# PSUM banks of the mixers dealt out anew: three for the projections, three for the HGRN, two for the mLSTM

## The chip, the cores and the metric

The kernel runs on one core of one Trainium2 chip. TensorE (PE) multiplies matrices and writes its results to PSUM, a memory of eight banks of 128 x 512 float32 each. VectorE (DVE) and ScalarE (ACT) read them from there; GpSimd (POOL) works on SBUF alone, and SyncE (SP) starts DMAs. The metric is the device time of one execution in microseconds; less is better. Where several runs were made their median is given.

## The reference

One residual block of a streaming encoder, 1024 tokens of width 1024, all in float32. What matters here is its first part, a mixer of two head groups that share one input projection:

```python
u = x @ w_in[i] + b_in[i]
hq, hf, hv, hgate, mq, mk, mv, mo, mig, mfg = _split_cols(u)
...
o_hg = hgrn2_mixer(silu(hq), log_f, k_hg, hv)            # 4 heads, 128 x 128 state
o_hg = head_rms_norm(o_hg, hg_norm_g[i]) * silu(hgate)
...
h_ml = mlstm_mixer(mq_c, mk_c, mv, mig, log_sigmoid(mfg)) # 4 heads, qk 64, v 128
o_ml = head_rms_norm(h_ml, ml_norm_g[i]) * sigmoid(mo)
mix = concatenate([o_hg, o_ml], -1) @ w_out[i]
x = layer_norm(ALPHA * x + mix, ln1_g[i], ln1_b[i])
```

Of the mLSTM, one step over a chunk of tokens is:

```python
qk = einsum('bhtd,bhsd->bhts', q_, k_) * w_intra
num = einsum('bhts,bhsv->bhtv', qk, v_) + w_inter[..., None] * einsum('bhtd,bhdv->bhtv', q_, C_st)
den = sum(qk, -1) + w_inter * einsum('bhtd,bhd->bht', q_, n_st)
h = num / maximum(abs(den), exp(-m_t))[..., None]
...
C_new = w_old[..., None, None] * C_st + einsum('bhs,bhsd,bhsv->bhdv', ws, k_, v_)
```

After the mixer come a SwiGLU feed-forward layer with its own layer norm and a gated embedding.

## The kernel before

The kernel goes through four stages: the mixers (`mixers`, up to about 416 us of the span), the output projection with the first layer norm (`out_proj`), and the two halves of the feed-forward layer with the last gate (`ffn_up`, `ffn_down`). All projections are done in three matmuls per product (`mm3`, lines 88 to 90): each float32 operand is split into a high part and the rest, and high x high, high x rest and rest x high are added up in PSUM.

The mixers use all eight PSUM banks, dealt out in three groups by `bank(tag, shape, name)`: `ft` for the projections, `hg` for the HGRN, `ml` for the mLSTM. A tile that is asked for takes a free bank of its group; its first writer waits until the bank's former tile has been read for the last time.

Projections (`ft`): `f_tile` computes one 128-column tile of the projection for 512 tokens at a time, 24 matmuls into one bank, and then calls an `evac` that reads the bank (ACT and DVE). `tok_group` does the same for 256 columns of two token tiles, with one DVE addition (L250) as the reader. `hf_tile` reads its bank twice on ACT (L489, L490), `hq_tile` once on ACT and once on DVE (L503, L504), the gates at the end once on ACT (L634).

Between them runs the recurrent work, as Python generators. `f_tile` and `tok_group` call `pump()` in the middle and at the end of each group, and each call moves every stream on to its next `yield`. So in the code the PE work of the streams stands between groups of 12 or 24 projection matmuls.

The mLSTM (`ml`, lines 407 to 468) takes eight chunks of 128 tokens, one after the other, and for each chunk asks for seven banks (six in the last): two `pq` (scores, L425, read by L427), `pk` (transposed keys, L430, read by L432); after a `yield` two `pn` (numerators and denominators, L440 and L446), then `pst` (the state's increment, L457, read by L459). `rms` (lines 387 to 405) then reads the two `pn` again: squares on ACT (L390), their sum and four small steps on DVE, a power on POOL (L398), a step on DVE (L400), and L404, which writes the normalised output, once for each `pn`. After two more `yield`s `pt` (transposed output, L465) is read by four copies on ACT (L468), and the next chunk begins in the same call of `pump`.

The HGRN (`hg`) runs two streams at once for each head (`hgrn`, lines 512 to 608), with tiles `sc`, `pkt`, `hst`, `po` and `pt`, and the same `rms`.

The order in which each engine works through its instructions is laid out before the run by the framework's planner. It follows the order of the code, but may put an instruction whose operands or bank it expects later behind others that it expects to be ready. On the chip each engine then keeps to that order, and waits where something is late.

At the very start eight accumulators `tok0` to `tok7` hold one bank each (line 161), and are read by L223 and L218. The small tiles `pg`, `pl`, `pm` and `pc` for the mLSTM's gates (lines 286 to 321) use `ml` banks too.

Of the kernel before, what the change touches and what calls it, by code (L numbers as in the profile page):

```python
# [9 lines left out]
F32 = mybir.dt.float32  # L10
# [8 lines left out]
P = 128  # L19
S = 1024  # L20
D = 1024
NC = 8
# [27 lines left out]
def block_kernel(ctx, tc, a, out):  # L50
# [69 lines left out]
    with tc.tile_pool(reuse_waits="tile", name="wp", bufs=3) as wp:  # L120
        g.wp = wp
        g.wtile = weights(wp, 1056, 2, 3)
        with ExitStack() as es:
            mixers(g, es)
        ff = ExitStack()
        g.psC = ctx.enter_context(tc.tile_pool(reuse_waits="tile", name="psC", bufs=8, space=PSUM))
        g.fw = ff.enter_context(tc.tile_pool(reuse_waits="tile", name="fw", bufs=3, side="right"))
        g.fh = ff.enter_context(tc.tile_pool(reuse_waits="tile", name="fh", bufs=3, side="right"))
        g.fe = ff.enter_context(tc.tile_pool(reuse_waits="tile", name="fe", bufs=8, side="right"))
        with ExitStack() as es:  # L130
            out_proj(g, es)
# [7 lines left out]
def mixers(g, es):  # L139
# [4 lines left out]
    ps = es.enter_context(g.tc.tile_pool(reuse_waits="tile", name="psA", bufs=1, space=PSUM))  # L144

    def bank(tag, shape, name):
        return ps.tile(shape, F32, tag=tag, bufs={"ft": 2, "hg": 3, "ml": 3}[tag], name=name)

    xh, xl = [], []
    for b in range(2):  # L150
# [3 lines left out]
    warm = mx.tile([P, HB], F32, name="st", bufs=2)  # L154
    dve.memset(warm, 0.0)
    wb = bank("hg", [P, 512], "warm")
    for _ in range(2):
        pe.matmul(wb, warm[:, :P], warm, start=True, stop=True)

    gts = kc.tile([P, NC, 8], F32)  # L160
    accs = [bank(("ml", "ft", "ft", "hg", "hg", "hg", "ml", "ml")[t], [P, 512], f"tok{t}") for t in range(NC)]

    def xs(t, k):
        tt = slice((t % 4) * P, (t % 4 + 1) * P)
# [75 lines left out]
    def tok_group(nm, off, dst, d0):  # L240
        hl = [wtile(a[nm][:, kk], 1024) for kk in range(2)]
        for t0 in range(0, NC, 2):
            acc = bank("ft", [P, 2, 256], "ft")
            for t in range(2):
                for k in range(KT):
                    mm3(acc[:, t], xs(t0 + t, k), ws(hl, k, 256), k == 0, k == KT - 1)
                if t == 0:
                    pump()
            vs = mx.tile([P, 2, 256], F32, name="st", bufs=2)
            dve.tensor_add(vs, acc, btok[:, None, off:off + 256].to_broadcast([P, 2, 256]))  # L250
            act.dma_start(dst[t0:t0 + 2, :, d0:d0 + 256].rearrange("t p n -> p t n"), vs)
            pump()
# [896 lines left out]
```

## Time and profile before

| | us |
|---|---|
| median of 3 runs | 1279.19 |
| lowest and highest | 1279.12, 1279.45 |
| the profiled execution | 1278.78 |
| its span, first to last instruction | 1277.0 |
| PE busy in the span | 1257.0 |
| DVE busy | 857.1 |
| ACT busy | 460.8 |
| POOL busy | 28.4 |

Of the profiled execution there is a page, and the trace behind it can be asked in other views: busy time by stretches, who waited for whom, all instructions on one tile, or a timeline. Times in them count from the start of the span. A line such as `113.64 0.44 PE L430 MATMUL pk<-c_ident,mqk 128*128 128x128 f32 x2` gives start, duration, engine, line of the kernel, operation, what is written and read, shapes, and how many alike follow each other; a bracket behind it gives the engine's idle time before it and what ended that. PE and PEld are TensorE's matmuls and its loads of stationary operands. Matmuls overlap in the pipeline, so the distance from one start to the next tells more than a duration. Views of one tile give the shortest, middle and longest duration in ns, and the first and last start.

### The profile page before, as it was taken

The page shows a single profiled execution, that of the slowest core. Times are in us where ns is not written, and L with a number is a line of the kernel's source. Part 1 is how long each engine was busy: PE and PEld are TensorE (multiplying, and loading weights), DVE is VectorE, ACT ScalarE, POOL GpSimd, SP SyncE. Part 2 cuts the span into 40 slices and gives each one's busy share as a digit, 9 for nine tenths or more (in the row PEclk, how much of TensorE's full clock was granted, in tenths as well). Part 3 has the DMA queues.
Part 4 walks back from the last instruction along what each step waited for, and adds up shares of the span by engine and source line. Part 5 has one row for each costly group of instructions (what it writes and reads, how often), then busy time and mean ns, then how long its engine had stood idle before and what let it go on. Part 6 is the DMA issues. An engine that isn't in the chain of part 4 may idle for free.

```text
span 1277.0 us, 19254 instructions
## 1 busy us (share of the span) xinstructions
PE 1257.0 (98%) x7795; PEld 1044.0 (82%) x7795; DVE 857.1 (67%) x1444; ACT 460.8 (36%) x663; POOL 28.4 (2%) x38
## 2 busy tenths in 40 slices
PE   9999999999999999899999999999999999999998
PEld 8799888777788887687788888888888888888887
DVE  7744665666533655578978778778757875559965
ACT  4671313223323414452333333333323533434141
POOL 0000000000000000000000000000000000000000
PEclk9999999999999999899999999999999999999999
DMA  7644412111112743525553443454448876555432
GB/s 245 185 129 137 126 52 67 44 42 51 35 33 105 291 165 134 192 87 190 189 190 141 164 159 146 149 189 157 149 148 320 311 248 205 193 182 170 168 124 75
DMA packets 90026, 194.35 MB, mean 152 GB/s; under 512 B 8721, under 2 KB 29137, under 8 KB 84177
## 3 DMA queue, kind: packets, MB, share of 16 engines
q1 hardware_dynamic: 55568, 134.10, 31.5%
q10 hardware_dynamic: 34368, 59.03, 12.6%
q8 instruction: 61, 1.00, 0.3%
q14 instruction: 29, 0.23, 0.1%
HBM read 142.47 MB, written 50.63 MB: 151 GB/s over the span
## 4 chain that ended last, share of the span: by engine, by line
PE 91%; DVE 5%; ACT 1%; issue 1%; POOL 1%; DMA 0%; ACTq 0%; SPq 0%; POOLq 0%
PE ft L88 8%; PE ft L89 7%; PE ft L90 7%; PE z L88 3%; PE z L90 3%; PE z L89 3%; PE x L88 3%; PE x L90 3%; PE y L90 3%; PE x L89 3%; PE y L88 3%; PE y L89 3%; PE dna L90 2%; PE dna L89 2%; PE pg L88 2%; PE pg L90 2%
## 5 line engine op out<-in xcount | busy, mean ns | idle before, releaser
L88 PE MATMUL ft<-xh,whl 128*128 128x512 f32 x320 | 129.2, 404 | 1.0 <-ACT k L490 1.0
L89 PE MATMUL ft<-xl,whl 128*128 128x512 f32 x320 | 127.3, 398 | 0.0
L90 PE MATMUL ft<-xh,whl 128*128 128x512 f32 x320 | 127.0, 397 | 0.0
L84 DVE TENSOR_TENSOR whl<-hw,whl 128x2048 fp32r<-128x2048 f32 (+1 forms) x42 | 88.4, 2106 | 54.7 <-ACT whl L83 54.7
L83 ACT CAST whl<-hw 128x2048 fp32r<-128x2048 f32 (+1 forms) x42 | 74.2, 1771 | 116.8 <-PE dna L90 39.8
L84 DVE TENSOR_TENSOR whl<-wraw,whl 128x1024 fp32r<-128x1024 f32 x62 | 75.2, 1218 | 51.4 <-ACT whl L83 51.2
L83 ACT CAST whl<-wraw 128x1024 fp32r<-128x1024 f32 x62 | 64.7, 1052 | 95.1 <-PE wo L90 40.7
L83 ACT CAST hl<-gu 128x1024 fp32r<-128x1024 f32 (+1 forms) x48 | 46.9, 981 | 79.1 <-PE x L90 62.5
L88 PEld LDWEIGHTS ft<-xh,whl 128*128 128x128 f32 x320 | 60.9, 190 | 15.3 <-ACT k L490 1.5
L90 PEld LDWEIGHTS ft<-xh,whl 128*128 128x128 f32 x320 | 60.1, 188 | 12.7
L88 PE MATMUL x<-XS,hl 128*128 128x512 f32 x176 | 68.7, 390 | 1.1 <-DVE p L861 1.1
L89 PEld LDWEIGHTS ft<-xl,whl 128*128 128x128 f32 x320 | 60.2, 188 | 11.7
L88 PE MATMUL z<-XA,hl 128*128 128x512 f32 x176 | 68.6, 390 | 0.0
L89 PE MATMUL z<-XA,hl 128*128 128x512 f32 x176 | 68.5, 389 | 0.0
L90 PE MATMUL x<-XS,hl 128*128 128x512 f32 x176 | 68.5, 389 | 0.0
L89 PE MATMUL x<-XS,hl 128*128 128x512 f32 x176 | 68.5, 389 | 0.0
L90 PE MATMUL dna<-whl 128*128 128x512 f32 x176 | 68.5, 389 | 0.0
L88 PE MATMUL dna<-whl 128*128 128x512 f32 x176 | 68.5, 389 | 0.0
L89 PE MATMUL dna<-whl 128*128 128x512 f32 x176 | 68.5, 389 | 0.0
L90 PE MATMUL z<-XA,hl 128*128 128x512 f32 x176 | 68.3, 389 | 0.0
L83 ACT CAST hl<-tt 128x1024 fp32r<-128x1024 f32 (+1 forms) x44 | 36.9, 838 | 64.5 <-PE w L90 26.7
L84 DVE TENSOR_TENSOR hl<-gu,hl 128x1024 fp32r<-128x1024 f32 (+1 forms) x48 | 54.2, 1132 | 6.1 <-ACT hl L83 6.1
(292 smaller groups left out, 3053.5 us busy)
## 6 DMA issues: line engine op xcount, KB each, us to landing
gu<-in_wgu SPq DMA_DIRECT2D x26, 1024.0 KB, 5.0
hw<-h_d SPq DMA_DIRECT2D x35, 512.0 KB, 4.0
wdp<-in_wd SPq DMA_DIRECT2D x11, 1024.0 KB, 4.8
h_d<-hs ACTq DMA_DIRECT2D x44, 256.0 KB, 3.5
wraw<-in_wf SPq DMA_DIRECT2D x20, 512.0 KB, 3.6
hw<-w_d SPq DMA_DIRECT2D x20, 512.0 KB, 5.1
w_d<-wdp ACTq DMA_DIRECT2D x33, 256.0 KB, 2.8
wraw<-in_wo SPq DMA_DIRECT2D x16, 512.0 KB, 3.3
```

What stands on the lines that cost most here:

```text
L83: g.act.copy(hi, raw)
L84: g.dve.tensor_sub(lo, raw, hi.bitcast(F32))
L88: g.pe.matmul(acc, lh, rh, start=first, stop=False, skip_group_check=more)
L89: g.pe.matmul(acc, lh, rl, start=False, stop=False, skip_group_check=more)
L90: g.pe.matmul(acc, ll, rh, start=False, stop=last, skip_group_check=more)
```

## The change

Two lines of `mixers` are changed. The projections get three banks instead of two, the mLSTM two instead of three; the HGRN keeps three. At the start the accumulator `tok6` goes to the `ft` group, so that the eight accumulators fit the new counts. The order of the code and all operations stay as they are.

```diff
     def bank(tag, shape, name):
-        return ps.tile(shape, F32, tag=tag, bufs={"ft": 2, "hg": 3, "ml": 3}[tag], name=name)
+        return ps.tile(shape, F32, tag=tag, bufs={"ft": 3, "hg": 3, "ml": 2}[tag], name=name)
...
-    accs = [bank(("ml", "ft", "ft", "hg", "hg", "hg", "ml", "ml")[t], [P, 512], f"tok{t}") for t in range(NC)]
+    accs = [bank(("ml", "ft", "ft", "hg", "hg", "hg", "ft", "ml")[t], [P, 512], f"tok{t}") for t in range(NC)]
```

## The prediction

> **What bounds the kernel now.** I read the page first: the busy time and the chain of work that ended last.
>
> ```profile
> span 1277.0 us, 19254 instructions
> ...
> PE 1257.0 (98%) x7795; PEld 1044.0 (82%) x7795; DVE 857.1 (67%) x1444; ACT 460.8 (36%) x663; POOL 28.4 (2%) x38
> ...
> PE 91%; DVE 5%; ACT 1%; issue 1%; POOL 1%; DMA 0%; ACTq 0%; SPq 0%; POOLq 0%
> ```
>
> TensorE (PE) sets the time. A time saved or lost on VectorE (DVE), ScalarE (ACT) or GpSimd (POOL) counts only where PE waits for it. So the next view is the busy time by stretches, over the part in which the mLSTM chunks run (100 to 210 us) and the rest of the mixers with the HGRN heads and the gates (210 to 420 us).
>
> ```profile
> 100.00:210.00 110.00, 107.44 (x1208) 94.82 (x1207) 65.94 (x231) 27.74 (x76) 8.31 (x8) 1.00 0.31 92
> 210.00:420.00 210.00, 206.14 (x2208) 167.40 (x2207) 113.02 (x290) 68.46 (x128) 8.54 (x8) 1.00 0.18 62
> ```
>
> The columns are the stretch, its length, then PE, weight loads, DVE, ACT, POOL, and the granted clock. PE is idle for 110.00 - 107.44 = 2.6 us and 210.00 - 206.14 = 3.9 us, 6.5 us together. All that bank counts could ever give back is in there. Who ended PE's waits, in the list of waits of PE over 0 to 425 us:
>
> ```profile
> PE sc L549 <- DVE k L571: 1.4, 2, 0.7
> PE ft L88 <- ACT k L490: 1.0, 2, 0.5
> PE sc L533 <- DVE onh L404: 0.9, 2, 0.5
> PE sc L533 <- DVE D L557: 0.7, 1, 0.7
> PE sc L533 <- DVE k L571: 0.7, 1, 0.7
> PE pk L430 <- ACT mix L468: 0.6, 3, 0.2
> PE wo L88 <- ACT st L634: 0.4, 1, 0.4
> PE pk L430 <- DVE Eall L427: 0.3, 1, 0.3
> ```
>
> Each row is who waited for whom, us in total, times, and the longest. Projections wait for a free ft bank only in the row ft L88 <- ACT k L490: two times in the whole stage, 1.0 us. The mLSTM waits for a free ml bank in the two rows of pk: 0.9 us. The three rows of sc with L557 and L571 are data, not banks.
>
> **The third ft bank.** It removes the 1.0 us: a projection group would have two groups of matmuls, not one, in which its bank can be emptied. Nothing else in the list names ft, so this part is worth -1.0 us (end on one side -1.3, with the step back to full pace; on the other 0, if ACT is late for other reasons). The Trainium skill, Perfetto Trace Analysis, section Matmuls, has independent groups rotate through different banks so that one group is emptied while the next is computed. By that rule the third bank helps and the mLSTM's lost bank hurts; the trace gives the first half a measured ceiling, the row of 1.0 us.
>
> **tok6.** It moves from an ml bank to an ft bank at the start. All eight are emptied by the same group of DVE additions:
>
> ```profile
> L218 DVE TENSOR_TENSOR vs<-tok,btok x8: 415/415/416, 26.4 to 30.6; 128x256 f32<-128x256 f32 x8
> L88 PE MATMUL ft<-xh,whl x320: 388/389/502, 28.7 to 415.5; 128*128 128x512 f32 x160
> L295 PE MATMUL pl<-c_ident,gg x2: 185/186/186, 39.0 to 39.1; 32*1 32x32 f32 x2
> ```
>
> The last begins at 30.6 us. The projections begin at 28.7 and reach their third bank two groups of 24 matmuls later; the mLSTM's second bank (pl) is first asked for at 39.0. I cost it at 0. The small gate tiles pg, pl, pm and pc now share two banks; each is made from what was read of the one before, so they were one chain already: 0. No DMA is moved, added or removed; each queue keeps its order.
>
> **The lost ml bank: pst.** This is the largest term. In one mLSTM step the code takes two banks pn and then, while both are alive, pst. The pn banks are last read by L404, at the end of rms. With two banks pst therefore can't start before the first L404 has ended. How long that is, in the timeline of chunk 0:
>
> ```profile
> 104.56 1.05 PE L440 MATMUL pn<-mv,Eall 128*128 128x129 f32 x8
> 105.54 0.66 PE L457 MATMUL pst<-mv,kws 128*64 128x129 f32 x8
> 106.25 0.35 DVE L459 SCALAR_TENSOR_TENSOR Cst<-Cst,wold,pst 128x129 f32<-128x129 f32 x1 [0.25 <-PE pst L457]
> ...
> 108.21 1.02 POOL L398 TENSOR_TENSOR rsm<-ssm,m 128x4 f32<-128x4 f32 x1 [106.49 <-DVE ssm L396]
> 109.26 0.16 DVE L400 TENSOR_TENSOR rsm<-rsm,den 128x4 f32<-128x4 f32 x1 [1.13 <-POOL rsm L398]
> 109.46 0.76 DVE L404 TENSOR_TENSOR onm<-pn,rsm 128x256 f32<-128x256 f32 x2
> ```
>
> pst starts at 105.54; the first L404 ends at about 109.46 + 0.42 = 109.9. So pst moves back by 4.3 us. Whether PE stands still for that depends on the order of its queue. The order is laid out by the planner before the run, and the trace shows what it does with an instruction that has no bank. In chunk 1, pk (next after pq in the code) has to wait for one:
>
> ```profile
> 112.42 0.72 PE L425 MATMUL pq<-mqk 64*128 64x128 f32 x8
> 113.07 0.39 PE L88 MATMUL ft<-whl,xh 128*128 128x256 f32 x1
> 113.29 0.28 PE L89 MATMUL ft<-whl,xh 128*128 128x256 f32 x1
> 113.64 0.44 PE L430 MATMUL pk<-c_ident,mqk 128*128 128x128 f32 x2
> 113.84 0.37 PE L90 MATMUL ft<-whl,xl 128*128 128x256 f32 x1
> ```
>
> Two projection matmuls were put ahead of it. So I expect the same for pst: projection matmuls fill the 4.3 us, and pst stands in the middle of a group. But PE's queue is fixed then, and where the chip is later than the plan PE stands. 113.29 to 113.64 is 0.35 us where such matmuls otherwise start some 0.12 us apart: 0.23 lost. How late the chip is behind the plan after the long way through rms, two other rows tell:
>
> ```profile
> 172.27 0.16 DVE L400 TENSOR_TENSOR rsm<-rsm,den 128x4 f32<-128x4 f32 x1 [0.90 <-POOL rsm L398]
> ...
> 174.92 0.46 PE L533 MATMUL sc<-q,k 128*32 128x32 f32 x32 [0.74 <-DVE k L571]
> ...
> 276.72 0.27 PE L533 MATMUL sc<-q,k 128*32 128x32 f32 x9 [0.46 <-DVE onh L404]
> ```
>
> At 276.72 PE waits 0.46 us for a bank that the HGRN's own L404 sets free: the same route. At 174.92 it stands 0.74 us on DVE work queued behind the mLSTM's L400. Ahead of that L400 DVE had idled for POOL, which it does in all eight chunks:
>
> ```profile
> DVE rsm L400 <- POOL rsm L398: 8.3, 8, 1.1
> ```
>
> 8.3 / 8 = 1.04 us each. That bounds the wait of pst: 0.46 below and 1.04 above, or nothing at all if the plan is slower than the chip here, which neither row suggests. I take 0.74, the row behind the mLSTM's own rms. Each break of a projection group costs 0.1 more: the first matmul after it takes 0.39 instead of 0.28 (113.07 against 113.29). There are 7 pst (none in the last chunk): 7 x 0.84 = **+5.9 us**, bounds 7 x 0.56 = 3.9 and 7 x 1.14 = 8.0. Behind pst in PE's queue stands the rest of the projection group, and all later PE work is late by as much. On DVE, L459 now waits for pst behind the L404s. That delays the HGRN's DVE work behind it in chunks 5 to 7 by up to 0.4 us each (the 0.66 us of pst less the rest of L404); DVE is busy for 65.94 of 110 us, so I cost it at 0, and at +1.2 if nothing covers it.
>
> A credit: the wait at 174.92 and its like in the next chunk (sc <- D L557, 0.7) came from the lag of the same route. If PE has already stood for it at pst, they go: **-1.5 us**, between 0 and -1.5.
>
> **The lost ml bank: pq and pk.** At the turn of a chunk pt, pq, pq and pk follow each other. With three banks pk waits for pt's bank (ACT mix L468) or the first pq's (DVE Eall L427). With two, the second pq waits for pt's, and pk for the first pq's. The first is an exchange of the same wait, 0. The second is new, but mostly passes while PE waits for pt's bank. Bounds: 0, and 8 x 0.35 (the 0.3 row of pk with a short step) = 2.8. I take 0.15 for each: **+1.2 us**.
>
> **The hand-over to the output projection.** wo L88 waits 0.4 us (the row above) for the bank of the last projection, which ACT reads:
>
> ```profile
> L634 ACT ACTIVATE st<-ft,c_fbias x16: 681/688/692, 319.3 to 416.6; 128x512 f32<-128x512 f32 x16
> ```
>
> With three ft banks another one of wo's banks is the last to come free: -0.4 if it is asked for later, +0.7 (one such reading more) if first. I take 0.
>
> **Sum.** -1.0 + 5.9 - 1.5 + 1.2 = **+4.6 us** on the profiled execution, whose time is 1278.8 us (span 1277.0). That execution is 0.4 us under the median of the runs, 1279.19, so I put the sum on the median: **1283.8 us**. All low ends: -1.3 + 3.9 - 1.5 + 0 - 0.4 = +0.7; all high ends: 8.0 + 1.2 + 2.8 + 0.7 = +12.7.
>
> **Rivals.**
> (1) No change, 1279 us. The plan is late enough that pst's bank is free when PE gets there. Then pst costs only 7 x 0.1, pk little, and ft gives its 1.0 back. For it: PE stands for pk for 0.2 or 0.3 at most. Against it: 0.46 and 0.74 in the rows behind rms. From a wait of 0.25 us or less for each pst the sum is within 0.2%.
> (2) Faster, 1276 us. One mechanism, at pst: it is put so far back that it never waits, and the three data waits of sc (2.8 us in the list) go since DVE's queue is laid out anew with L459 behind L404; with the 1.0 of ft that is some -3. It decides from the point where pst waits nothing and at least two thirds of the sc waits go. Against it: those waits follow from POOL's 1.04 us, which stay.
> (3) Much slower, about 1309 us. PE holds pst in its place: 7 x 4.3 = 30 us. Against it: pk at 113.64 was passed by; and DVE's queue would hold L459 ahead of L404, which could never end. The Trainium skill, TensorE: Matmul & The Clock Gate, section on psum-queue depth-cycling, says that idling between groups while banks are cycled makes the clock fall back. By the trace that takes longer waits than mine: with the 0.74 waits in it the stretch 100 to 210 has a granted clock of 1.00. The one stretch with a lower clock is this:
>
> ```profile
> 520.00:540.00 20.00, 15.05 (x72) 12.00 (x71) 6.12 (x9) 12.39 (x19) 0.52 (x1) 0.85 0.52 190
> ```
>
> PE is idle for 5 us there. Holding pst could do the same seven times, at 20 x 0.15 = 3 us each: about 1330 us, the tail of this rival.
>
> That the change doesn't do what it says can be in one sense: ft may hardly use its third bank, since it waited for one twice only. That moves the sum by 1.0 at most and lies in rival (1).
>
> **How the numbers follow.** A measurement of this kernel can tell about 0.2%, 2.6 us, from no change. My forecast (slower by more than that, with pst as its main term) has 0.64, no change 0.27, faster 0.06, much slower 0.03. The range reaches from 1277.8, a little under rival (1), to 1290, near the high ends: it leaves out most of rivals (2) and (3) and the far tail of the sum. Faster 0.06, same 0.27, slower 0.67.
>
> **What would show it.** In the changed kernel's timeline pst no longer follows pn but stands between ft matmuls some 4 us later, with an idle time before it that ends at DVE onm L404; 0.5 to 1.0 us in each of seven chunks proves the main term, under 0.25 refutes it. The wait of ft for L490 is gone from the list. DVE's L459 stands behind L404. The second pq waits for ACT mix L468. PE's idle time in 100 to 210 us grows from 2.6 to some 7 us. I am wrong if PE's waits there grow by less than 2 us, or if the time moves outside the mixers, after 420 us, where nothing was changed.

## The result, and the profile after

The changed kernel takes 1287.76 us (median of 4 runs, 1286.77 to 1289.34), the kernel before 1279.32 us in the same comparison. The ratio is 1.0068, with a 95% interval of 1.0056 to 1.0080: slower by some 8.5 us. The forecast was slower, 1283.8 us, with a range of 1277.8 to 1290.0; the way and the range were right, the loss is nearly twice the forecast of 4.6 us.

The page of the changed kernel, whose profiled execution took 1287.79 us:

```profile
span 1286.0 us, 19266 instructions
...
PE 1262.6 (98%) x7795; PEld 1047.6 (81%) x7795; DVE 859.6 (67%) x1444; ACT 460.2 (36%) x663; POOL 28.1 (2%) x38
```

The span is 9.0 us longer, and PE's share of it has not moved. Of these 9.0 us, 5.6 are longer busy time of PE for the same 7795 matmuls (1262.6 against 1257.0), and 3.4 are idle time (1286.0 - 1262.6 = 23.4 against 20.0). So the loss is not waiting alone: some matmuls take longer. The first matmul of the output projection marks the end of the mixers. The group of that tile, before and after (the last two times are the first and the last start):

```profile
L88 PE MATMUL wo<-whl,mixh x128: 389/389/497, 416.2 to 508.8; 128*128 128x512 f32 x128
```

```profile
L88 PE MATMUL wo<-whl,mixh x128: 389/389/499, 425.6 to 518.7; 128*128 128x512 f32 x128
```

The output projection starts 9.4 us later (425.6 against 416.2), and the span is 9.0 us longer: all of the loss is in the mixers, and the stages behind them take 0.4 us less. The busy time by stretches of the changed kernel:

```profile
100.00:210.00 110.00, 102.02 (x1119) 88.21 (x1118) 61.90 (x210) 23.09 (x65) 7.18 (x7) 1.00 0.29 90
210.00:420.00 210.00, 208.10 (x2262) 170.26 (x2261) 111.15 (x296) 64.23 (x122) 9.33 (x9) 1.00 0.15 47
```

In the stretch of the mLSTM chunks PE's idle time went from 2.6 to 8.0 us; in the stretch of the HGRN it fell from 3.9 to 1.9. The waits of PE over 0 to 440 us name the cause:

```profile
PE pst L457 <- DVE onm L404: 7.9, 7, 1.3
PE warm L158 <- DVE st L155: 1.5, 1, 1.5
PE sc L533 <- DVE onh L404: 1.3, 2, 0.6
PE sc L533 <- issue: 0.4, 1, 0.4
PE wo L88 <- ACT st L634: 0.4, 1, 0.4
```

Seven waits of pst for a bank of pn, 7.9 us. The waits of ft for L490, of pk, and those of sc for L571 and L557, all in the list of before, are gone; those of sc for L404 grew from 0.9 to 1.3 us. The timeline of chunk 0:

```profile
108.54 1.02 POOL L398 TENSOR_TENSOR rsm<-ssm,m 128x4 f32<-128x4 f32 x1 [106.83 <-DVE ssm L396]
...
109.17 0.28 PE L88 MATMUL ft<-whl,xh 128*128 128x256 f32 x1
109.59 0.16 DVE L400 TENSOR_TENSOR rsm<-rsm,den 128x4 f32<-128x4 f32 x1 [1.13 <-POOL rsm L398]
109.79 0.75 DVE L404 TENSOR_TENSOR onm<-pn,rsm 128x256 f32<-128x256 f32 x2
110.36 0.66 PE L457 MATMUL pst<-mv,kws 128*64 128x129 f32 x8 [0.91 <-DVE onm L404]
110.95 0.38 PE L89 MATMUL ft<-whl,xh 128*128 128x256 f32 x1
...
111.06 0.35 DVE L459 SCALAR_TENSOR_TENSOR Cst<-Cst,wold,pst 128x129 f32<-128x129 f32 x1 [0.52 <-PE pst L457]
```

pst stands in the middle of a projection group, behind the L88 of 109.17, and that group goes on at 110.95. In between PE stands 0.91 us, for the last 0.1 us of POOL's step and then for DVE's L400 and first L404. L459 now comes behind the L404s. All of this is as the forecast had it.

A second change was not in the forecast in this form. PE's timeline at the turn from chunk 0 to 1:

```profile
113.94 0.71 PE L425 MATMUL pq<-mqk 64*128 64x128 f32 x4
114.58 0.39 PE L88 MATMUL ft<-whl,xh 128*128 128x256 f32 x1
...
115.37 0.71 PE L425 MATMUL pq<-mqk 64*128 64x128 f32 x4
116.01 0.38 PE L90 MATMUL ft<-whl,xl 128*128 128x256 f32 x1
```

Before, the eight short matmuls of both pq took from 112.42 to 113.07, 0.65 us. Now the second pq needs pt's bank, five projection matmuls were put ahead of it, and each half takes 0.64 us by itself (113.94 to 114.58, 115.37 to 116.01). PE is not idle for it in any view; it is part of the 5.6 us of longer busy time. All seven later chunks have their pq in two such pieces. Added up from start to start, without idle time, the pq matmuls of the eight chunks take 5.4 us before and 9.6 us now.

### The profile page after: what moved, and what is told of

Same layout as the page of the kernel before. It is cut to its first block, busy times and chain, and to the rows that moved or that the text cites. A ratio compares the mean times of both kernels' runs of the same rounds, so it can differ in the third digit from the quotient of the medians.

```text
span 1286.0 us, 19266 instructions
## 1 busy us (share of the span) xinstructions
PE 1262.6 (98%) x7795; PEld 1047.6 (81%) x7795; DVE 859.6 (67%) x1444; ACT 460.2 (36%) x663; POOL 28.1 (2%) x38
## 4 chain that ended last, share of the span: by engine, by line
PE 90%; DVE 5%; ACT 2%; issue 1%; POOL 1%; DMA 1%; SPq 0%; ACTq 0%; POOLq 0%
PE ft L88 7%; PE ft L89 7%; PE ft L90 7%; PE z L88 3%; PE z L90 3%; PE z L89 3%; PE x L88 3%; PE x L90 3%; PE x L89 3%; PE y L90 3%; PE y L88 3%; PE y L89 3%; PE pg L88 2%; PE dna L89 2%; PE dna L88 2%; PE dna L90 2%
## 5 line engine op out<-in xcount | busy, mean ns | idle before, releaser
L88 PE MATMUL ft<-xh,whl 128*128 128x512 f32 x320 | 129.4, 404 | 0.0
L88 PEld LDWEIGHTS ft<-xh,whl 128*128 128x128 f32 x320 | 60.8, 190 | 13.7 <-issue 0.2
L88 PE MATMUL x<-XS,hl 128*128 128x512 f32 x176 | 68.6, 390 | 0.6 <-DVE p L861 0.6
L88 PE MATMUL z<-XA,hl 128*128 128x512 f32 x176 | 68.6, 390 | 0.0
L88 PE MATMUL dna<-whl 128*128 128x512 f32 x176 | 68.5, 389 | 0.0
```

The costliest lines, as they stand in the source:

```text
L88: g.pe.matmul(acc, lh, rh, start=first, stop=False, skip_group_check=more)
```

## The experiments

Theory A: PE stands for pst's bank because its queue was laid out as if pn were free earlier than it is. Against it: B, the split pq and the other new breaks cost it; C, the new order of the HGRN's work does.

**e1, pst moved behind the second yield.** Banks as in the change.

```diff
-        if c < NC - 1:
-            pst = bank("ml", [P, 2, VW], "pst")
-            ...
         on = rms("m", views, den)
         yield
         yield
+        if c < NC - 1:
+            pst = bank("ml", [P, 2, VW], "pst")
+            ...
```

> The changed kernel with the block of pst and Cst moved behind the second yield of the mLSTM step, where both pn have long been read; banks 3, 3, 2 as in the change. Theory A (PE stands for pst's bank, 7.9 us of waits and some 0.2 us of break for each of seven): the wait of PE for pst on DVE onm L404 falls from 7.9 us to under 0.5, and the time falls by 8 to 9 us, to 1278 to 1281. Rival B (the splitting of pq and pk by the second bank, and breaks of the projection groups in general): the wait may go, but the time stays above 1284. Rival C (the loss comes with the changed order of the HGRN's DVE work): 1283 or more, with longer waits of sc.

Measured: 1279.21 us, ratio to the kernel before 1.0004 (0.9995 to 1.0014). The waits of PE hold no pst:

```profile
PE warm L158 <- DVE st L155: 1.5, 1, 1.5
PE sc L533 <- DVE onh L404: 1.3, 2, 0.6
PE sc L533 <- issue: 1.0, 1, 1.0
PE wo L88 <- ACT st L634: 0.4, 1, 0.4
```

From 1.0068 to 1.0004 are some 8 us (0.0064 x 1279): as A has it, and neither B nor C. Some 1 us of it may be pq, which stays apart at four of the seven turns here, not at all seven, and takes 8.5 us in sum instead of 9.6; e4 below has no such doubt.

**e2, the same move with the old banks.**

```diff
-bufs={"ft": 3, "hg": 3, "ml": 2}
+bufs={"ft": 2, "hg": 3, "ml": 3}
```

> The kernel before (banks 2, 3, 3) with the same block moved behind the second yield. It is the yardstick for the run before it: what the move does without the new banks. Theory A: pst never waited here, so within 1.5 us of the kernel before (1278 to 1281), and the run with the new banks lies within 2 us of this one. Rival B: this one is 3 us or more under the run with the new banks, since pq is not split here.

Measured: 1281.07 us, ratio 1.0016 (1.0007 to 1.0026), just outside the 1281 expected. The move itself costs some 2 us where pst did not wait, and with it the new banks are not behind the old ones (1.0004 against 1.0016). The waits that the third ft bank removes are there:

```profile
PE sc L549 <- DVE k L571: 1.4, 2, 0.7
PE sc L533 <- DVE k L571: 1.2, 1, 1.2
PE ft L88 <- ACT k L490: 1.0, 2, 0.5
```

**e3, the projections back at two banks.** The third serves tok6 alone.

```diff
-bufs={"ft": 3, "hg": 3, "ml": 2}
+bufs={"ft": 2, "hg": 3, "ml": 2, "own": 1}
...
-("ml", "ft", "ft", "hg", "hg", "hg", "ft", "ml")
+("ml", "ft", "ft", "hg", "hg", "hg", "own", "ml")
```

> The changed kernel with the projections back at two banks; the third one serves tok6 at the start only and lies idle afterwards. It prices the third ft bank alone. Theory A: the two waits of ft on ACT k L490 come back (about 1.0 us, 1.5 with the step back to full pace), so 1 to 2 us over the changed kernel, 1288.5 to 1290; pst waits 7 to 9 us as in the changed kernel. Rival C (the third ft bank itself changes the order for the worse): 3 us or more under the changed kernel.

Measured: 1289.38 us, ratio 1.0083 (1.0068 to 1.0098). The interval overlaps that of the change, so the trace has to give the size:

```profile
PE pst L457 <- DVE onm L404: 7.9, 7, 1.3
PE warm L158 <- DVE st L155: 1.5, 1, 1.5
PE sc L549 <- DVE k L571: 1.4, 2, 0.7
PE ft L88 <- ACT k L490: 1.0, 2, 0.5
```

pst waits as long as with three banks for the projections. What returns is the 1.0 us of ft, and the 1.4 us of sc L549 as well. This second wait is in every run with two ft banks (before, e2, e3, e8) and in none with three; how the bank acts on it was not taken apart. Against these 2.4 us, e3's list has 0.4 us less of sc for L404 (0.9 against 1.3) and 0.4 us less of wo. By time the bank is worth 1.6 us (1289.38 - 1287.76) or 1.9 (from the ratios), so some 2 us, not 1.0.

**e4, pst in a bank of the projections**, in its old place in the code.

```diff
-            pst = bank("ml", [P, 2, VW], "pst")
+            pst = bank("ft", [P, 2, VW], "pst")
```

> The changed kernel, but pst takes a bank of the projections instead of one of the mLSTM; its place in the code is as it was. Theory A: pst does not need a pn bank any more, its wait on L404 is gone and it follows pn again; 1279 to 1283, where what is left over the kernel before is the split pq (some 3 us) less what ft and sc gain. Rival B: 1285 or more. A projection may now wait for pst's bank: up to 0.5 us in seven chunks.

Measured: 1279.47 us, ratio 1.0006 (0.9996 to 1.0015). Again about 8 us less, now with the code's order untouched: A. pst follows pn again, and its wait is gone from the list:

```profile
105.11 1.05 PE L440 MATMUL pn<-mv,Eall 128*128 128x129 f32 x8
106.10 0.66 PE L457 MATMUL pst<-mv,kws 128*64 128x129 f32 x8
```

pq is still in two pieces at all seven turns and takes 9.6 us in sum as in the change, so the 8 us are not B's. Two of its waits are of interest:

```profile
PE sc L533 <- DVE k L571: 0.7, 1, 0.7
PE sc L533 <- DVE D L557: 0.7, 1, 0.7
```

These two, the credit of the forecast, are there when pst does not wait in its old place (before, e4, e10) and gone when it does (the change, e3). In e5 below, where POOL has no part in the mLSTM, they are gone too: both fit the lag that the forecast named. It is no rule for other orders of the code: in e1 pst does not wait, and yet they are gone, while sc has one wait of 1.0 us without a named cause.

**e5, the power left out of the mLSTM's rms.** DVE copies the mean square in its place, so the mLSTM's output is scaled otherwise and POOL has no part in it.

```diff
-        pool.tensor_tensor(rs, ss, g.m8[:, :4], op=OP.pow)
+        if scale_r is not None:
+            dve.tensor_copy(rs, ss)
+        else:
+            pool.tensor_tensor(rs, ss, g.m8[:, :4], op=OP.pow)
```

> The changed kernel with the power left out of the mLSTM's rms: DVE copies the mean square in its place, so POOL has no part in the mLSTM (its output is scaled otherwise; the HGRN's rms is whole). It tells what the 1.13 us are made of for which PE waits at each pst. Theory A (PE's queue was laid out as if POOL's step took far less than its 1.02 us): the waits of pst fall from 7.9 us to under 2.5, and the time by 5 to 8 us against the changed kernel, to 1280 to 1283. Rival D (the lag builds up over all the small steps of rms): the waits stay at 5 us or more, the time at 1285 or more.

Measured: 1280.67 us, ratio 1.0015 (1.0005 to 1.0024). The wait in its list (three lines further down in this kernel):

```profile
PE pst L460 <- DVE onm L407: 1.1, 4, 0.4
```

From 7.9 to 1.1 us: most of the wait was POOL's step, 6.8 / 7 = 0.97 us of it on average.

**e6, the power done twice on POOL**, the second time into the same place.

```diff
         pool.tensor_tensor(rs, ss, g.m8[:, :4], op=OP.pow)
         if scale_r is not None:
+            pool.tensor_tensor(rs, ss, g.m8[:, :4], op=OP.pow)
```

> The changed kernel with the power of the mLSTM's rms done twice on POOL, the second time into the same place: one more step of 1.02 us in the way to L404 in each of eight chunks. Theory A: PE's wait for pst grows by nearly as much, from 1.13 to some 2 us each, 14 us in all, and the time by 5 to 8 us, to 1293 to 1296. Rival D: the queue is laid out with the second step in mind, the waits grow by less than 0.3 us each and the time by less than 3 us.

Measured: 1300.95 us, ratio 1.0178 (1.0162 to 1.0193). Its wait, and its stretches with the granted clock (third number from the end):

```profile
PE pst L459 <- DVE onm L406: 14.9, 7, 2.4
```

```profile
100.00:140.00 40.00, 35.81 (x274) 33.16 (x272) 15.80 (x49) 5.16 (x14) 4.05 (x4) 0.91 0.31 102
140.00:180.00 40.00, 33.87 (x182) 25.88 (x179) 20.49 (x73) 9.18 (x21) 6.05 (x6) 0.96 0.31 96
180.00:220.00 40.00, 35.32 (x612) 32.06 (x610) 22.76 (x82) 6.97 (x22) 4.44 (x4) 0.91 0.13 41
```

The waits grew by 7.0 us, 1.0 for each chunk: once more the whole of a step on POOL. The place of pst in PE's queue did not move with it: from the start of the last pn matmul to that of the first of pst, without idle time, PE has 3.6 to 4.9 us of work, by chunk, in the change, in e5 and in e6 alike (within 0.3 us chunk by chunk). So the queue was laid out as if a step that takes 1.02 us took as good as nothing. The time grew by 13.2 us, not by 5 to 8 as expected: the granted clock is 0.91 to 0.96 in these stretches, where the changed kernel has 1.00 from 100 to 210 us. The page has PE busy for 1270.1 us against 1262.6 in the change, with the same matmuls: 7.5 us, about what the waits leave open. A lower clock fits that (40 x 0.09 + 40 x 0.04 + 40 x 0.09 = 8.8 us, an estimate from the three rows), but how the time divides between the clock and the rest was not tried.

**e7 and e9, e1 with the second pq in a bank of the projections**, to keep pq in one piece.

```diff
-            pq = bank("ml", [P, 2, P], "pq")
+            pq = bank("ft" if q else "ml", [P, 2, P], "pq")
```

> The kernel with the new banks and pst behind the second yield (e1), and the second pq of each chunk in a bank of the projections. It prices the splitting of pq. Theory A: pq stays in one piece, which saves up to 3 us of short steps (14 more breaks of PE's row of work at some 0.2 us), so 1276 to 1278. Rival E: the pieces cost nothing in sum, since the projections go on between them; within 1 us of e1 (1278 to 1280.5).

> The kernel of e7 once more, with five rounds: new banks, pst behind the second yield, the second pq in a bank of the projections. Theory A (with pst's wait and the splitting of pq gone, the third ft bank's 1.5 us and the sc waits that went with it are left as a gain): 1 to 2 us under the kernel before, with an interval below 1.0. Otherwise it is no better than the kernel before, within 0.05%.

Measured: 1277.35 us, ratio 0.9992 (0.9982 to 1.0001), and 1277.62 us, ratio 0.9994 (0.9985 to 1.0003) in the second set of runs. The first time lies where A put it, but not for A's reason. With pst and pt ahead in both ml banks it is now the first pq that waits, and the pieces stay apart at four of the seven turns (timeline of e7 at the first):

```profile
112.52 0.71 PE L425 MATMUL pq<-mqk 64*128 64x128 f32 x4
113.16 0.38 PE L88 MATMUL ft<-whl,xh 128*128 128x256 f32 x1
113.48 0.71 PE L425 MATMUL pq<-mqk 64*128 64x128 f32 x4
```

In e1 it is four turns as well, and the pq matmuls take 8.5 us in sum in both kernels, so e7 says nothing about the price of the split. What it gained over e1, some 1.5 us by the ratios, was not taken apart. As a kernel it can't be told from the one before.

**e8, e1 with the free bank given to the HGRN.**

```diff
-bufs={"ft": 3, "hg": 3, "ml": 2}
+bufs={"ft": 2, "hg": 4, "ml": 2}
...
-("ml", "ft", "ft", "hg", "hg", "hg", "ft", "ml")
+("ml", "ft", "ft", "hg", "hg", "hg", "hg", "ml")
```

> pst behind the second yield as in e1, but the bank freed by the mLSTM goes to the HGRN instead of the projections: two, four, two. Theory A: PE's waits of sc on the HGRN's onh L404 (1.3 us) go, the waits of ft (1.0) and of sc L549 (1.4) that the third ft bank had taken away come back: 1 to 2 us over e1, 1280 to 1281.5. Rival F (the HGRN's banks are what counts): 2 us or more under e1.

Measured: 1280.32 us, ratio 1.0011 (1.0001 to 1.0020): some 1 us over e1, within A's range, though the intervals of the two overlap; only rival F is ruled out by the time. The waits are A's: the HGRN's wait on L404 is gone; those of the projections and of sc L549 are back, and a wait without a named cause of 1.6 us has come:

```profile
PE sc L533 <- issue: 1.6, 2, 1.4
PE warm L158 <- DVE st L155: 1.5, 1, 1.5
PE sc L549 <- DVE k L571: 1.4, 2, 0.7
PE ft L88 <- ACT k L490: 1.0, 2, 0.5
```

**e10, pst and the second pq in banks of the projections**, both in their old places.

```diff
-            pq = bank("ml", [P, 2, P], "pq")
+            pq = bank("ft" if q else "ml", [P, 2, P], "pq")
...
-            pst = bank("ml", [P, 2, VW], "pst")
+            pst = bank("ft", [P, 2, VW], "pst")
```

> New banks, pst in its old place but in a bank of the projections, and the second pq in one too. Theory A: no wait of pst, pq in one piece, no more breaks of the projections than before the change; 1276 to 1279. Rival G (three banks for the projections are too few once pst and pq share them): waits of ft or pst for a bank of 2 us or more in sum, 1280 or more.

Measured: 1276.50 us, ratio 0.9980 (0.9972 to 0.9989), faster than both kernels. At the turn of the chunk pq is in one piece, and pk has its short wait of before:

```profile
112.40 0.72 PE L425 MATMUL pq<-mqk 64*128 64x128 f32 x8
113.05 0.39 PE L88 MATMUL ft<-whl,xh 128*128 128x256 f32 x1
113.27 0.28 PE L89 MATMUL ft<-whl,xh 128*128 128x256 f32 x1
113.63 0.44 PE L430 MATMUL pk<-c_ident,mqk 128*128 128x128 f32 x2
```

Its list of waits has no ft, no pst and no sc L549. Against e4, which differs in pq alone, it is 0.0026 x 1279 = 3.3 us faster (each ratio against the kernel before on the same chip). The pieces explain that: 7 x 0.64 = 4.5 us for the second halves, less the 0.9 us of pk's waits, which are back. The pages agree, e4 first:

```profile
PE 1259.9 (99%) x7795; PEld 1046.9 (82%) x7795; DVE 857.6 (67%) x1444; ACT 460.5 (36%) x663; POOL 28.1 (2%) x38
```

```profile
PE 1255.9 (99%) x7795; PEld 1043.3 (82%) x7795; DVE 856.6 (67%) x1444; ACT 460.7 (36%) x663; POOL 28.1 (2%) x38
```

PE is busy for 4.0 us less, and pq takes 5.4 us in sum instead of 9.6.

## Why the forecast was right, and where it was short

- **What bounds it.** Right: PE, in the mixers; all that follows takes 0.4 us less in sum.
- **pst, +5.9 us.** The mechanism was right to the line, and rival (3), PE holding pst in its place, did not occur. The size was short. Of two rows that bounded the wait I took 0.74, PE's wait for DVE work behind the mLSTM's L400, and put POOL's 1.04 as the upper end. Measured were 7.9 / 7 = 1.13, from 0.91 to 1.34: the waits alone are 7.9 us, and with 0.1 for each break 8.6, over the upper end of 8.0. e5 and e6 show what it should have gone by: each step on POOL adds its full duration to the wait, as if it had no place in the plan. That row of before, DVE idle for 8.3 us behind POOL in all eight chunks, pointed there. By e4 the whole of pst, with its credit, is some 8 us, where the forecast had 5.9 - 1.5 = 4.4.
- **The credit, -1.5 us.** Right for this order of the code: both waits of sc are gone, and e4 has them back.
- **pq and pk, +1.2 us.** The step failed in kind. I priced a second wait of pk; but pk's waits went, and the cost is that pq falls in two. e10 against e4 puts it at 3.3 us, over the upper end of 2.8. The rows were at hand: the two projection matmuls ahead of pk showed what the planner does, and the first was not asked what a pq costs when it stands alone.
- **The third ft bank, -1.0 us.** The wait went as said. It took the wait of sc L549 along, 1.4 us that I had held for data only, and made others longer; some 2 us are left by e3, past the -1.3 at the end of the range.
- **tok6 and the hand-over, 0.** Right: wo's wait is still 0.4 us.

With these sizes the sum is 8 for pst with its credit, 3.3 for pq, -2 for the third bank: about +9 us, against 8.5 measured by the medians. e4, e10 and e3 were measured one by one and share a little, so the agreement is no finer than 1 or 2 us. That the time fell inside the range is in part luck: the range was wide, three of its terms left their own bounds, and the third bank's error took back some of the other two.

## What to carry to other kernels

Before a pool of banks is cut, look for the point in the code where most of its tiles are alive at once: a tile asked for there will wait for the last reader of the others, however far down the code that stands. Where the order of a queue is laid out beforehand, the price of such a wait need not be the distance it moves (4.3 us here); in this kernel it was what the plan had left out of the way there (one step on POOL, 1.0 us). And a bank that a busy stage has to spare can serve a tile of the stage that is short, as pst and the second pq did here, for a gain of 0.2% where the cut alone lost 0.7%.

## What the runs showed of the hardware

Two short matmul groups on different halves of the partitions (64 rows each) cost 0.65 us side by side and 0.64 us each when other matmuls come between them. Side by side, in chunk 1 of the kernel before, they start in pairs 0.014 us apart; in a piece that stands alone, no two start less than 0.11 us apart. The Trainium skill, TensorE: Matmul & The Clock Gate, section Packing small matmuls, says that matmuls on different row groups of the array overlap; the trace agrees, by these figures.

Waits of PE of 0.9 to 1.3 us, seven in 90 us, left the granted clock at 1.00; seven of 2.1 us on average in e6 (14.9 / 7, the longest 2.4) went with 0.91 to 0.96 in each stretch of 40 us that held them. Where between these a wait begins to cost clock, and whether the longest or the sum of them decides, no run here shows.
